# The up-projection of a conv-FFN by one level of Strassen's scheme, on an input that is normed first, with two tensors sent through DRAM

## Chip, cores and metric

One of the eight cores of a Trainium2 chip runs the whole program as one launch. The metric is the device time of one execution in microseconds, median of the runs; the profile is of one further execution. A core has TensorE (matmuls, PE below; its weight loads are listed apart as PEld), VectorE (DVE), ScalarE (ACT), GpSimd (POOL) and SyncE (SP), whose queue issues all of this kernel's DMAs. Each engine works through its own instruction list in order and waits on semaphores.

## The reference, cut to what matters

One decoder layer for 512 prompt tokens and 8 x 8 sample tokens that share all weights, 576 columns in all (`NT`). After four mixers, `w_out` and a cross-attention comes the FFN; this is the part that changes:

```python
def conv_ffn(xn, buf, w_up, conv_w, w_down):
    hup = xn @ w_up                                  # 2048 -> 11264 = 2 x 5632
    hc, new_buf = causal_dwconv(hup, buf, conv_w)    # width 3, along the tokens
    u, g = jnp.split(hc, 2, axis=-1)
    return (jax.nn.silu(g) * u) @ w_down, new_buf    # 5632 -> 2048

f, ffn_buf_new = conv_ffn(rmsnorm(x, lp['g_ffn']), ffn_buf, lp['w_up'], lp['ffn_conv_w'], lp['w_down'])
x = x + f
y = rmsnorm(x, g_final)
```

All inputs are fp32.

## The kernel before, in words

Activations lie transposed: 128 channels on the partitions, 576 tokens along the row. To keep fp32 accuracy in fp32r matmuls, each operand is split into a rounded half `hi` (ScalarE, L123) and a remainder `lo` (VectorE, L124, `lo = raw - hi`), and a product is three matmuls: hi by hi, hi by lo, lo by hi. A matmul has 128 x 128 weights and 288 moving columns, half of the tokens, so a 128 x 128 block of a weight array costs 6 matmuls (`linear`, L151). Weights come as tiles `raw` of 512 KB (512 rows by 256 columns, L119), in two buffers, and their halves in two buffers each.

The program is written once, and a scheduler orders each engine's instructions ahead of time by levels of priority (`at("evac")`, `at("weights")`, `at("drain")`, `at("mix")`, `at("fill")`, from high to low). What the chip runs is that fixed order.

The stages that matter here are these. `cross` ends with two halves of `w_mem_o`, whose sums are added to x in SBUF (`xT`, L303). In the second half `add_x("g_ffn")` also makes the FFN's input `xh`, `xl` (x times the gain; L305, L306) and sums the squares for the norm (ScalarE squares, GpSimd adds, L310). The factor 1/rms, `self.r`, is made by `row_rstd` (L323 to L329) and is applied later: `conv` multiplies each 128 x 576 result of `w_up` by it as it leaves PSUM (L507, L508). So the matmuls of `w_up` need not wait for the norm.

`ffn` goes over 11 blocks of 4 x 128 channels of u and of g. `up` makes 256 columns of u, then 256 of g; `conv` adds the state columns (GpSimd, L510), copies out the new state (GpSimd, L515, L516) and does the width-3 convolution (L521, L523); silu(g) u is split into the halves `mh`, `ml` (L332, L333), which stay in SBUF. `down(blk - 1)` is scheduled behind `up(blk)`: 16 column blocks x 4 x 6 matmuls, added to `xT` (L303). The last 4 channel blocks of `w_down` are done in `final` together with the last norm and the output (L602, L604).

PSUM has 8 banks: two accumulators `acc` of two banks each and four single banks.

Of the kernel before, what the change touches and what calls it, by code (L numbers as in the profile page):

```python
# [284 lines left out]
class Post(Net):  # L285
    def add_x(self, g=None, first=False):

        nc = self.nc
# [171 lines left out]
    def ffn(self):  # L460
        nc, tc, a, o = self.nc, self.tc, self.a, self.o
        NB = 4
        ah, al = {}, {}
# [2 lines left out]
        def down(blk):
            self.linear(ah.pop(blk), al.pop(blk), a["w_down"][0], 0, 2048, self.add_x(), k0=NB * blk, nk=NB)

        n = 44 // NB
        with ExitStack() as c:  # L470
            fp = c.enter_context(tc.tile_pool(name="fp", bufs=2, side="right"))
            f1 = c.enter_context(tc.tile_pool(name="f1", bufs=1, side="right"))
            st = f1.tile([128, 88, 16], F32, name="st")
            with self.at("mix"):

                raw = fp.tile([128, 1408], F32, name="sraw", bufs=1)
                nc.sync.dma_start(raw, bass.AP(tensor=a["state_ffn_conv"].tensor, offset=0, ap=[[1408, 8], [11264, 16], [1, 1408]]))
                s4 = st.rearrange("p (g j) r -> p g j r", g=8)
                for q in range(0, 11, 4):
                    m = min(4, 11 - q)  # L480
# [1 line left out]
                    for j in range(m):
                        nc.tensor.transpose(p[:, 128 * j:128 * j + 128], raw[:, 128 * (q + j):128 * (q + j) + 128], self.ident)
                    for j in range(m):
                        nc.vector.tensor_copy(s4[:, :, q + j], p[:, 128 * j:128 * j + 128].rearrange("p (g r) -> p g r", g=8))
            bufs = [f1.tile([128, 594], F32, name=f"ub{i}") for i in range(4)]
            for b in bufs:
                nc.gpsimd.memset(b, 0.0)
            outs, full = {}, []

            def states(ready):

                with self.at("fill"):
                    for g in ready:
                        p = self.pm()
                        nc.tensor.transpose(p[:72, :128], outs[g].rearrange("p r f -> p (r f)"), self.ident)
                        w = fp.tile([72, 128], F32, name="cw", bufs=2)
                        nc.scalar.copy(w, p[:72, :128])
                        for n, z in (("p_ffn_conv", w[:8]), ("s_ffn_conv", w[8:])):
                            nc.sync.dma_start(rows(n)[:, 512 * g:512 * g + 512].rearrange("r (f c) -> r f c", f=4), z)  # L500

            def conv(ft, ps, slot):

                u = bufs[slot]
                smp = u[:, 514:594].rearrange("p (b t) -> p b t", b=8)
                with self.at("evac"):
                    nc.vector.tensor_tensor(u[:, 2:514], ps[:, :512], self.r[:, :512], op=OP.mult)  # L507
                    nc.vector.tensor_tensor(smp[:, :, 2:10], ps[:, 512:].rearrange("p (b t) -> p b t", b=8),  # L508
                                            self.r[:, 512:].rearrange("p (b t) -> p b t", b=8), op=OP.mult)
                nc.gpsimd.tensor_copy(smp[:, :, 0:2], st[:, ft].rearrange("p (b t) -> p b t", b=8))  # L510
                g = ft // 4
                if ft % 4 == 0:
                    outs[g] = fp.tile([128, 18, 4], F32, name="co", tag=f"co{slot // 2}", bufs=2)
                co = outs[g]
                nc.gpsimd.tensor_copy(co[:, 0:2, ft % 4], u[:, 512:514])  # L515
                nc.gpsimd.tensor_copy(co[:, 2:18, ft % 4].rearrange("p (b t) -> p b t", b=8), smp[:, :, 8:10])  # L516
                if ft % 4 == 3:
                    full.append(g)
                y = fp.tile([128, 592], F32, name="y", tag=f"y{slot // 2}", bufs=2 - slot // 2)
                w = lambda k: self.v("ffn_conv_w", 88 * k + ft)  # L520
                nc.scalar.activation(y, u[:, :592], AF.Copy, scale=w(0))  # L521
                for k in (1, 2):
                    nc.vector.scalar_tensor_tensor(y, u[:, k:k + 592], w(k), y, op0=OP.mult, op1=OP.add)  # L523
                return y

            def up(blk):
                h, l = ah.setdefault(blk, {}), al.setdefault(blk, {})
                for pair in range(0, NB, 2):
                    ys = {}

                    def done_u(i, ps):
                        ys[i] = conv(NB * blk + pair + i, ps, i)

                    def done_g(i, ps):
                        j = NB * blk + pair + i
                        y = conv(44 + j, ps, 2 + i)
                        s = fp.tile([128, 592], F32, name="s", bufs=1)
                        nc.scalar.activation(s, y, AF.Silu)
                        t = fp.tile([128, NT], F32, name="t", bufs=1)
                        yu = ys[i]  # L540
                        nc.vector.tensor_tensor(t[:, :512], s[:, :512], yu[:, :512], op=OP.mult)
                        v = [z[:, 512:592].rearrange("p (b t) -> p b t", b=8)[:, :, 2:10] for z in (s, yu)]
                        nc.vector.tensor_tensor(t[:, 512:].rearrange("p (b t) -> p b t", b=8), v[0], v[1], op=OP.mult)
                        h[pair + i] = self.wo.tile([128, 604], F32R, name="mh", tag="mh", bufs=6)[:, :NT]
                        l[pair + i] = self.wo.tile([128, 604], F32R, name="ml", tag="ml", bufs=6)[:, :NT]
                        self.halves(h[pair + i], l[pair + i], t)
                    ready, full[:] = full[:], []
                    self.linear(self.xh, self.xl, a["w_up"][0], 128 * (NB * blk + pair), 256, done_u)
                    states(ready)
                    self.linear(self.xh, self.xl, a["w_up"][0], 5632 + 128 * (NB * blk + pair), 256, done_g)  # L550

            for blk in range(n):
                up(blk)
                if blk < n - 1 and blk:
                    down(blk - 1)
            down(n - 2)
            states(full)
        return ah.pop(n - 1), al.pop(n - 1)

    def final(self, fh, fl, fw, fo):  # L560

        nc, a, o = self.nc, self.a, self.o
# [5 lines left out]
        for c in range(0, 2048, 256):
            with self.at("weights"):
                raw = fw.tile([128, 4, 256], F32, name="raw", bufs=2)  # L570
                nc.sync.dma_start(raw, w[5120:, c:c + 256].rearrange("(k p) c -> p k c", p=128))
                nc.scalar.copy(wh[:, :, c:c + 256], raw)
# [1460 lines left out]
```

## Time and profile before

| | us |
|---|---|
| median of 3 runs (lowest, highest) | 3131.99 (3126.44, 3134.4) |
| the profiled execution's own time | 3129.54 |
| its span, from the first to the last instruction | 3127.7 |
| PE busy in the span | 3010.8 (96%) |
| DVE busy | 1715.1 (55%) |
| ACT busy | 962.6 (31%) |
| POOL busy | 437.0 (14%) |

A matmul is counted busy from its start to its modelled end, and matmuls overlap, so the rate of work is read from counts per stretch. The FFN runs from 1414 us (the first matmul of `w_up`) to 3055 us, `final` from there to the end. The granted TensorE clock is 0.988 of full speed over the span.

### The profile page before, as it was taken

To read this page: it belongs to the slowest core of one execution; us is meant where nothing else is said; L and a number is where in the kernel's file an instruction comes from. 1 tells how busy PE (TensorE), PEld (TensorE's weight loads), DVE (VectorE), ACT (ScalarE), POOL (GpSimd) and SP (SyncE) were. 2 spreads that over 40 slices of the span, in tenths; PEclk is the share of its full clock that TensorE was granted. 3 is DMA by queue.
4 is the path that set the end of the run, shared out by engine and by line. 5 is a ranking of instruction groups with operands and counts; after the bars stand their busy time and mean duration, and the time that the engine had idled before them with its cause. 6 is when DMAs were issued, how large, how long until landed. Compare 5 with 4: busy or idle time off the path is not lost.

```text
span 3127.7 us, 53649 instructions
## 1 busy us (share of the span) xinstructions
PE 3010.8 (96%) x22323; PEld 2867.6 (92%) x22323; DVE 1715.1 (55%) x2878; ACT 962.6 (31%) x1612; POOL 437.0 (14%) x563
## 2 busy tenths in 40 slices
PE   8998989999999999989999999999999999999998
PEld 8888977887888789879999999999999999999997
DVE  7857766778666666465443434444444444444454
ACT  4433322343332444233221222222222222222233
POOL 4111422313211003021110100000000000000000
PEclk9999999999999999999999999999999999999999
DMA  5455566545575553322222222222222222222232
GB/s 165 136 182 156 169 179 183 150 149 160 166 222 156 189 185 113 108 77 82 82 83 83 88 82 82 82 89 81 83 82 89 82 83 81 89 82 82 82 123 75
DMA packets 350587, 368.28 MB, mean 118 GB/s; under 512 B 35846, under 2 KB 298715, under 8 KB 349640
## 3 DMA queue, kind: packets, MB, share of 16 engines
q1 hardware_dynamic: 350344, 364.84, 37.3%
q8 instruction: 176, 2.88, 0.4%
q14 instruction: 67, 0.55, 0.1%
HBM read 320.44 MB, written 46.99 MB: 117 GB/s over the span
## 4 chain that ended last, share of the span: by engine, by line
PE 80%; DVE 8%; DMA 7%; issue 2%; ACT 1%; SPq 1%; POOL 1%; DVEq 0%; ACTq 0%; POOLq 0%
PE acc L151 68%; PE acc L602 2%; DVE lo L129 2%; DMA old<-in_cache_win_k 1%; PE acc L194 1%; PE pm L1395 1%; DMA od<-acc 1%; PE pm L926 1%; DMA kn<-in_cache_win_k 1%; DVE acc L877 1%; DMA raw<-in_w_down 1%; DMA old<-in_cache_win_v 1%; PE pm L805 1%; DMA dw<-dn 0%; DMA raw<-in_w_in 0%
## 5 line engine op out<-in xcount | busy, mean ns | idle before, releaser
L151 PE MATMUL acc<-xh,hi 128*128 128x288 f32 x4224 | 921.2, 299 | 20.3 <-DVE nt L1055 13.8
L151 PE MATMUL acc<-xl,hi 128*128 128x288 f32 x4224 | 923.3, 298 | 2.7 <-DVE xl L245 2.7
L151 PE MATMUL acc<-xh,lo 128*128 128x288 f32 x4224 | 914.9, 299 | 2.9 <-DVE lo L129 2.8
L124 DVE TENSOR_TENSOR lo<-raw,hi 128x1024 fp32r<-128x1024 f32 x322 | 397.2, 1233 | 594.6 <-ACT hi L123 588.1
L151 PEld LDWEIGHTS acc<-xh,hi 128*128 128x128 f32 x4224 | 686.0, 190 | 33.0 <-issue 25.1
L151 PEld LDWEIGHTS acc<-xl,hi 128*128 128x128 f32 x4224 | 687.6, 190 | 10.6 <-issue 6.8
L151 PEld LDWEIGHTS acc<-xh,lo 128*128 128x128 f32 x4224 | 684.0, 190 | 10.3 <-issue 4.9
L123 ACT CAST hi<-raw 128x1024 fp32r<-128x1024 f32 x322 | 337.9, 1049 | 1093.0 <-PE acc L151 1002.2
L151 PE MATMUL acc<-mh,hi 128*128 128x288 f32 x1920 | 421.7, 300 | 8.3 <-DVE xT L303 7.1
L151 PE MATMUL acc<-mh,lo 128*128 128x288 f32 x1920 | 416.9, 297 | 0.2 <-DVE lo L124 0.2
L151 PE MATMUL acc<-ml,hi 128*128 128x288 f32 x1920 | 416.0, 296 | 0.0
L303 DVE TENSOR_TENSOR xT<-acc,xT 128x576 f32<-128x576 f32 x240 | 181.2, 756 | 275.4 <-PE acc L151 274.8
L151 PEld LDWEIGHTS acc<-mh,hi 128*128 128x128 f32 x1920 | 308.3, 189 | 17.0 <-DVE xT L303 8.5
L151 PEld LDWEIGHTS acc<-ml,hi 128*128 128x128 f32 x1920 | 310.1, 189 | 3.9 <-issue 3.2
L151 PEld LDWEIGHTS acc<-mh,lo 128*128 128x128 f32 x1920 | 309.0, 189 | 3.5 <-issue 2.9
L515 POOL COPY co<-ub 128x2 f32<-128x2 f32 x88 | 61.0, 694 | 1291.3 <-DVE ub L507 1291.3
L128 ACT ACTIVATE hi<-raw,gmix 128x256 fp32r<-128x256 f32 x320 | 136.5, 498 | 212.2 <-PE acc L151 160.0
L129 DVE SCALAR_TENSOR_TENSOR lo<-raw,gmix,hi 128x256 fp32r<-128x256 f32 x320 | 171.9, 582 | 45.7 <-ACT hi L128 45.1
L523 DVE SCALAR_TENSOR_TENSOR y<-ub,vec,y 128x592 f32<-128x592 f32 x176 | 146.4, 832 | 42.6 <-ACT y L521 40.3
L521 ACT ACTIVATE y<-ub,vec 128x592 f32<-128x592 f32 x88 | 69.7, 792 | 157.9 <-DVE ub L508 156.0
L507 DVE TENSOR_TENSOR ub<-acc,sq 128x512 f32<-128x512 f32 x88 | 60.6, 688 | 53.9 <-PE acc L151 53.9
L1395 PE MATMUL pm<-dw 128*128 128x128 f32 (+1 forms) x456 | 61.8, 282 | 9.0 <-DVE dw L1409 5.3
(645 smaller groups left out, 2770.7 us busy)
## 6 DMA issues: line engine op xcount, KB each, us to landing
raw<-in_w_up SPq DMA_DIRECT2D x176, 512.0 KB
raw<-in_w_down SPq DMA_DIRECT2D x88, 512.0 KB
raw<-in_w_in SPq DMA_DIRECT2D x80, 512.0 KB
raw<-in_w_out SPq DMA_DIRECT2D x32, 512.0 KB
old<-in_cache_win_k SPq DMA_DIRECT2D x48, 256.0 KB
old<-in_cache_win_v SPq DMA_DIRECT2D x48, 256.0 KB
kn<-in_cache_win_k SPq DMA_DIRECT2D x32, 256.0 KB
v<-in_cache_win_v SPq DMA_DIRECT2D x32, 256.0 KB
```

Of the source, the lines that this page charges most:

```text
L123: nc.scalar.copy(hi, raw)
L124: nc.vector.tensor_tensor(lo, raw, hi, op=OP.subtract)
L128: nc.scalar.activation(hi[:, k], raw[:, k], AF.Copy, scale=g)
L129: nc.vector.scalar_tensor_tensor(lo[:, k], raw[:, k], g, hi[:, k], op0=OP.mult, op1=OP.subtract)
L151: nc.tensor.matmul(acc[m][:, 224 + 288 * j:512 + 288 * j], wt[:, k, 128 * m:128 * m + 128], at(x, kb + k)[:, 288 * j:288 * j + 288], start ...
L303: nc.vector.tensor_tensor(x, ps, old, op=OP.add)
L507: nc.vector.tensor_tensor(u[:, 2:514], ps[:, :512], self.r[:, :512], op=OP.mult)
L515: nc.gpsimd.tensor_copy(co[:, 0:2, ft % 4], u[:, 512:514])
L521: nc.scalar.activation(y, u[:, :592], AF.Copy, scale=w(0))
L523: nc.vector.scalar_tensor_tensor(y, u[:, k:k + 592], w(k), y, op0=OP.mult, op1=OP.add)
L602: nc.tensor.matmul(ps, x[k][:, tok], z[:, k, cs], start=k == 0 and i == 0, stop=k == 3 and i == 2)
L1395: nc.tensor.matmul(p[:n, n * h:n * h + n], lhs[:, h], rhs[:, h], start=True, stop=True)
```

## The change: what it does

`w_up` is multiplied by one level of Strassen's scheme (in the form with shared sums). A group is 2 row blocks x 2 column blocks of `w_up` (128 x 128 each) by 2 row blocks x 2 token halves of the input; 8 products of 128 x 128 x 288 become 7. The 7 products of each group accumulate in PSUM over the 8 groups of a 256-column pair, so the sums of products are done once a pair. One product is still three matmuls.

- `add_x(out=True)` no longer makes `xh`, `xl`; it writes each block of x to DRAM (`xd`) and sums the squares.
- `ffn_x` (new) starts when `self.r` is there: it reads x back (`z`), multiplies by gain and 1/rms, makes the four sums of the input blocks (three on GpSimd, one on VectorE) and splits all 7 operands, `Xh[q]`, `Xl[q]`, which stay in SBUF.
- `up_pair` (new) replaces `linear` for `w_up`: of each `raw` tile GpSimd makes the four sums `S` (4 instructions of 128 x 256); the halves are made in three pieces of 512, 256 and 1024 columns (`ah`/`al` from `raw`, `hi`/`lo` from `S`). The seven accumulators take seven banks: two `acc` and three of the four single banks; the fourth is left for the states. After the last of four chunks, ScalarE copies P1 (`t1`) and VectorE makes the four results (L538 to L544, and `sums`, L607 to L610), straight into the convolution's buffers `ub`, without the factor 1/rms.
- silu(g) u goes to DRAM (`hx`, one DMA of 288 KB per block), not into halves.
- `ffn_down` (new) runs after all of `w_up`: 5 blocks of 8 channel blocks, each read back (`ht`, three buffers) and split; before it x is read back into a new `xT`. The last 4 are split for `final`, whose weights are now made in `final_weights` at the end of `ffn_down`.

The diff, cut to its core:

```diff
-    def add_x(self, g=None, first=False):
+    def add_x(self, g=None, first=False, out=False):
...
-            if g:
+            if out:
+                nc.sync.dma_start(self.xd[m], x)
+            elif g:
                 nc.scalar.activation(self.xh[:, m], x, AF.Copy, scale=self.v(g, m))
...
+    def ffn_x(self, xc, zs):
...
+        for q in range(8):
+            with self.at("evac"):
+                z = zs.tile([128, 2, NT], F32, name="z", bufs=2)
+                nc.sync.dma_start(z, self.xd[2 * q:2 * q + 2].rearrange("k p t -> p k t"))
+                for k in range(2):
+                    nc.vector.scalar_tensor_tensor(z[:, k], z[:, k], self.v("g_ffn", 2 * q + k), self.r, op0=OP.mult, op1=OP.mult)
+                t = zs.tile([128, 4, 288], F32, name="t", bufs=2)
+                b11, b12, b21, b22 = (z[:, k, 288 * j:288 * j + 288] for k in range(2) for j in range(2))
+                sub(nc.gpsimd, t[:, 0], b12, b11)
+                sub(nc.gpsimd, t[:, 1], b22, t[:, 0])
+                sub(nc.vector, t[:, 2], b22, b12)
+                sub(nc.gpsimd, t[:, 3], t[:, 1], b21)
+                h, l = self.Xh[q], self.Xl[q]
+                self.halves(h[:, 0], l[:, 0], b11)
+                self.halves(h[:, 1:3].rearrange("p a b -> p (a b)"), l[:, 1:3].rearrange("p a b -> p (a b)"), z[:, 1])
+                self.halves(h[:, 3:], l[:, 3:], t)
+    def up_pair(self, sp, w, c0, done):
+        prods = {"P1": (("a", 0), 0), "P2": (("a", 1), 1), "P4": (("a", 2), 6), "P5": (("s", 0), 3), "P6": (("s", 1), 4), "P7": (("s", 2), 5), "P3": (("s", 3), 2)}
+        for ch in range(4):
+            with self.at("weights"):
+                raw = self.wp.tile([128, 4, 256], F32, tag="raw", name="raw", bufs=2)
...
+                g = nc.gpsimd.tensor_tensor
+                g(S[:, 0], A(2, 1), A(2, 2), op=OP.add)
+                g(S[:, 1], S[:, 0], A(1, 1), op=OP.subtract)
+                g(S[:, 2], A(1, 1), A(2, 1), op=OP.subtract)
+                g(S[:, 3], A(1, 2), S[:, 1], op=OP.subtract)
...
+                self.halves(ah[:, :2], al[:, :2], both)
+                self.halves(ah[:, 2], al[:, 2], A(2, 2))
+                self.halves(sh, sl, S)
...
+                        for j, (wt, xx) in enumerate(((hi, xh), (hi, xl), (lo, xh))):
+                            nc.tensor.matmul(P[name], wt[:, i, q], xx, start=ch == 0 and q == 0 and j == 0, stop=ch == 3 and q == 1 and j == 2)
+                if ch == 3:
+                    with self.at("evac"):
...
+                            nc.vector.tensor_tensor(u2, t1, P["P6"], op=OP.add)
...
+                            nc.vector.tensor_tensor(t1, u2, P["P7"], op=OP.add)
+                            done(0, 1, OP.subtract, t1, P["P4"])
+                            done(1, 1, OP.add, t1, P["P5"])
+                            nc.vector.tensor_tensor(u2, u2, P["P5"], op=OP.add)
...
+                nc.sync.dma_start(self.hx[j + n], t)
...
+        for blk in range(5):
+            ps = [parts(NB * blk + k, hp, 11) for k in range(NB)]
+            self.linear({k: p[0] for k, p in enumerate(ps)}, {k: p[1] for k, p in enumerate(ps)}, a["w_down"][0], 0, 2048, self.add_x(), k0=NB * blk, nk=NB)
```

How the instructions stand. First VectorE's list in the middle of the FFN. Before, one 256-column half of u (`ub` is the convolution's buffer, `lo` the weights' remainder, line numbers those of the kernel before):

```order
L507 TENSOR_TENSOR ub_15175<-acc,sq 128x512
L508 TENSOR_TENSOR ub_15175<-acc,sq 128x8x8
L523 SCALAR_TENSOR_TENSOR y<-ub_15175,vec,y 128x592 x2
L507 TENSOR_TENSOR ub_15176<-acc,sq 128x512
L508 TENSOR_TENSOR ub_15176<-acc,sq 128x8x8
L124 TENSOR_TENSOR lo<-raw,hi 128x1024
L523 SCALAR_TENSOR_TENSOR y<-ub_15176,vec,y 128x592 x2
L124 TENSOR_TENSOR lo<-raw,hi 128x1024 x3
```

After the change, the end of one pair and the start of the next (line numbers of the changed kernel; L337 is `halves`, `pp` and `acc` are the products in PSUM):

```order
L538 TENSOR_TENSOR u_21630<-t_21603,pp 128x288
L607 TENSOR_TENSOR ub_15312<-t_21603,acc 128x288
L541 TENSOR_TENSOR t_21603<-u_21630,pp 128x288
L337 TENSOR_TENSOR al<-raw,ah 128x512
L337 TENSOR_TENSOR al<-raw,ah 128x256
L607 TENSOR_TENSOR ub_15313<-t_21603,acc 128x288
L609 TENSOR_TENSOR ub_15313<-t_21603,acc 128x224
L610 TENSOR_TENSOR ub_15313<-t_21603,acc 128x8x8
L544 TENSOR_TENSOR u_21630<-u_21630,acc 128x288
L337 TENSOR_TENSOR lo<-S,hi 128x1024
L609 TENSOR_TENSOR ub_15312<-u_21630,pp 128x224
L610 TENSOR_TENSOR ub_15312<-u_21630,pp 128x8x8
```

The weights' remainder is in three pieces per chunk, and instructions on sums in PSUM stand between the pieces of the next pair's second chunk.

Second, VectorE at the start of the FFN. Before, the last evacuations of `w_mem_o` and the norm stand among the FFN's first weights:

```order
L303 TENSOR_TENSOR xT<-acc,xT 128x576
L306 SCALAR_TENSOR_TENSOR xl<-xT,vec,xh 128x576
L124 TENSOR_TENSOR lo<-raw,hi 128x1024
L306 SCALAR_TENSOR_TENSOR xl<-xT,vec,xh 128x576
L124 TENSOR_TENSOR lo<-raw,hi 128x1024
L324 TENSOR_SCALAR nt<-pm 128x288 x2
L326 RECIPROCAL sq<-nt 128x288 x2
```

After the change, the norm (L328 to L333, which are L324 to L329 before), and then the input's operands (`z`, `t`, `Xl`) among the first weights (`al`, `lo`):

```order
L333 SCALAR_TENSOR_TENSOR sq<-nt,sq 128x288 x2
L337 TENSOR_TENSOR al<-raw,ah 128x512
L337 TENSOR_TENSOR al<-raw,ah 128x256
L337 TENSOR_TENSOR al<-raw,ah 128x512
L337 TENSOR_TENSOR al<-raw,ah 128x256
L478 SCALAR_TENSOR_TENSOR z<-z,vec,sq 128x576 x2
L337 TENSOR_TENSOR Xl_15151<-z,Xh_15150 128x288
L472 TENSOR_TENSOR t<-z 128x288
L478 SCALAR_TENSOR_TENSOR z<-z,vec,sq 128x576 x2
L337 TENSOR_TENSOR Xl_15151<-z,Xh_15150 128x576
L337 TENSOR_TENSOR lo<-S,hi 128x1024
```

The DMA of the first `z` waits for the last instruction of the norm, since its buffer takes the place of the norm's own buffers.

Third, the SP queue where `w_up` ends and `w_down` begins. Before, the two kinds of weights alternate:

```order
L119 DMA raw<-in_w_up 128x4x256 x9
L119 DMA raw<-in_w_down 128x4x256 x3
L500 DMA out_p_ffn_conv<-cw 2x4x128
L500 DMA out_s_ffn_conv<-cw 16x4x128
L119 DMA raw<-in_w_down 128x4x256
```

After the change, the last two blocks of silu(g) u, the four parts of x, and the blocks that are read back:

```order
L627 DMA hx<-t 128x576
L2098 DMA xT<-xd 128x4x576 x4
L627 DMA hx<-t 128x576
L638 DMA ht<-hx 128x576 x12
L119 DMA raw<-in_w_down 128x4x256
```

The read-back of x stands ahead of the last write of `hx` and of every read of `ht`. Its first DMA waits for the last instruction that reads the last `ub` (L600), and the first `ht` waits until the last write of `hx` has landed and the last silu is done, by the places of the buffers in SBUF.

## Rows read from the trace of the kernel before

**Rows 1.** Page: span, and the busy time of each engine.

```profile
span 3127.7 us, 53649 instructions
PE 3010.8 (96%) x22323; PEld 2867.6 (92%) x22323; DVE 1715.1 (55%) x2878; ACT 962.6 (31%) x1612; POOL 437.0 (14%) x563
```

**Rows 2.** Windows: length, busy us (count) of PE, PEld, DVE, ACT, POOL; clock, DMA, GB/s.

```profile
1430.00:3000.00 1570.00, 1570.00 (x11819) 1569.67 (x11818) 676.44 (x867) 384.05 (x437) 114.54 (x258) 1.00 0.26 84
```

**Rows 3.** Chain that ended last, 1774 to 1928 us: start, us, link.

```profile
1780.72 146.68 PE acc L151 x1104
```

**Rows 4.** Groups by shape, 1430 to 3000 us: count, busy, mean ns, idle before.

```profile
L151 PEld LDWEIGHTS acc<-xh,hi 128*128 128x128 f32 x2780 | 447.8, 189 | 0.0
...
L124 DVE TENSOR_TENSOR lo<-raw,hi 128x1024 fp32r<-128x1024 f32 x246 | 301.3, 1225 | 565.6 <-ACT hi L123 561.1
L523 DVE SCALAR_TENSOR_TENSOR y<-ub,vec,y 128x592 f32<-128x592 f32 x174 | 144.7, 832 | 42.6 <-ACT y L521 40.3
L333 DVE TENSOR_TENSOR ml<-t,mh 128x576 fp32r<-128x576 f32 x42 | 31.7, 755 | 6.6 <-ACT mh L332 6.6
L541 DVE TENSOR_TENSOR t<-s,y 128x512 f32<-128x512 f32 x42 | 28.9, 689 | 10.3 <-ACT s L538 10.0
L508 DVE TENSOR_TENSOR ub<-acc,sq 128x64 f32<-128x64 f32 x87 | 18.7, 215 | 0.0
L328 DVE TENSOR_TENSOR nt<-nt 128x288 f32<-128x288 f32 x1 | 0.5, 451 | 0.0
L510 POOL COPY ub<-st 128x16 f32<-128x16 f32 x84 | 16.9, 201 | 176.3 <-DVE y L523 176.3
```

**Rows 5.** Timeline of VectorE, 3009 to 3012 us: start, us, instruction.

```profile
3010.05 1.22 DVE L124 TENSOR_TENSOR lo<-raw,hi 128x1024 fp32r<-128x1024 f32 x1
3011.18 0.75 DVE L303 TENSOR_TENSOR xT<-acc,xT 128x576 f32<-128x576 f32 x1
```

**Rows 6.** Groups of GpSimd by shape, 60 to 95 us.

```profile
L1535 POOL TENSOR_TENSOR cm<-W 128x256 f32<-128x256 f32 x1 | 1.1, 1084 | 0.0
L1534 POOL TENSOR_TENSOR cm<-W,W 128x256 f32<-128x256 f32 x1 | 0.7, 658 | 0.1
```

**Rows 7.** Timelines of VectorE and GpSimd, 349 to 364 us, both without a pause.

```profile
351.30 5.20 DVE L129 SCALAR_TENSOR_TENSOR lo<-raw,gmix,hi 128x256 fp32r<-128x256 f32 x4
363.71 0.49 DVE L129 SCALAR_TENSOR_TENSOR lo<-raw,gmix,hi 128x256 fp32r<-128x256 f32 x1 [0.33 <-ACT hi L128]
...
350.08 6.13 POOL L1897 TENSOR_TENSOR nt<-xh,xl 128x576 f32<-128x576 f32 x4 [1.50 <-DMA xd<-nt]
```

**Rows 8.** Windows: second half of `w_mem_o`, and a piece of it behind a wait.

```profile
1373.70:1414.40 40.70, 31.03 (x189) 29.22 (x190) 35.19 (x41) 22.55 (x34) 23.69 (x21) 0.88 0.20 58
1383.30:1386.90 3.60, 3.60 (x17) 3.60 (x16) 2.93 (x8) 0.58 (x1) 1.90 (x5) 0.50 0.01 2
```

**Rows 9.** Timelines from 1386 to 1433 us, GpSimd, PE and VectorE: squares, then the norm.

```profile
1390.84 1.43 POOL L310 TENSOR_TENSOR sq<-sq,nt 128x576 f32<-128x576 f32 x1 [0.64 <-ACT nt L308]
...
1422.24 1.13 PE L323 MATMUL pm<-sq,mean 128*128 128x288 f32 x4
...
1428.13 0.67 DVE L485 COPY st<-pm 128x128 f32<-128x128 f32 x3
...
1429.65 1.22 DVE L124 TENSOR_TENSOR lo<-raw,hi 128x1024 fp32r<-128x1024 f32 x1
...
1431.16 0.82 DVE L329 SCALAR_TENSOR_TENSOR sq<-nt,sq 128x288 f32<-128x288 f32 x2
```

**Rows 10.** Timelines of SP's queue and ScalarE, 3001 to 3007 us: a weight load and its reader.

```profile
3002.06 1.94 SPq L571 DMA_DIRECT2D raw<-in_w_down  x2
...
3005.74 1.05 ACT L572 CAST wh<-raw 128x1024 fp32r<-128x1024 f32 x1 [2.98 <-DMA raw<-in_w_down]
```

**Rows 11.** Windows of the first loads; the last number is GB/s.

```profile
3.00:5.00 2.00, 0.18 (x1) 0.08 (x1) 0.00 (x0) 0.17 (x1) 0.00 (x0) 1.00 0.87 328
11.00:13.00 2.00, 2.00 (x17) 2.00 (x15) 1.71 (x3) 1.60 (x4) 1.92 (x2) 1.00 1.04 434
```

More of the change, by code (lines that the diff above doesn't have):

```diff
@@ L456, in cross @@
             z = lambda y: {k: y[2 * pair + k] for k in range(2)}
-            self.linear(z(oh), z(ol), a["w_mem_o"][0], 0, 2048, self.add_x("g_ffn" if pair else None), k0=2 * pair, nk=2)
+            self.linear(z(oh), z(ol), a["w_mem_o"][0], 0, 2048, self.add_x(out=pair > 0), k0=2 * pair, nk=2)
         self.banks = (0, 1, 2, 3)
[L460 to L463, printed above, removed]
-        rows = lambda n: o[n].rearrange("a b k c -> (a b k) c")
[L466 to L480, printed above, removed]
-                    p = self.pm()
[L482 to L558, printed above, removed]
@@ L560, in final @@
-    def final(self, fh, fl, fw, fo):
+    def ffn_x(self, xc, zs):
+        nc = self.nc
+        B11, B21, B22, T1, T2, T3, T4 = range(7)
+        self.Xh, self.Xl = {}, {}
+        for q in range(7, -1, -1):
+            self.Xh[q] = xc.tile([128, 7, 288], F32R, name=f"Xh{q}")
+            self.Xl[q] = xc.tile([128, 7, 288], F32R, name=f"Xl{q}")
+        sub = lambda e, o, x, y: e.tensor_tensor(o, x, y, op=OP.subtract)
+        for q in range(8):
[14 more added lines that the diff above has]
+                self.halves(h[:, 3:], l[:, 3:], t)
@@ new lines, in ffn_down, with parts @@
+    def ffn_down(self, hp, hs, last):
+        nc, a = self.nc, self.a
+        NB = 8
+        def parts(j, pool, bufs):
+            with self.at("drain"):
+                t = hs.tile([128, NT], F32, name="ht", bufs=3)
+                nc.sync.dma_start(t, self.hx[j])
+                h, l = (pool.tile([128, NT], F32R, name=f"h{z}", bufs=bufs) for z in "hl")
+                self.halves(h, l, t)
+                return h, l
+        for blk in range(5):
+            ps = [parts(NB * blk + k, hp, 11) for k in range(NB)]
+            self.linear({k: p[0] for k, p in enumerate(ps)}, {k: p[1] for k, p in enumerate(ps)}, a["w_down"][0], 0, 2048, self.add_x(), k0=NB * blk, nk=NB)
+        ps = [parts(40 + k, last, 4) for k in range(4)]
+        return [p[0] for p in ps], [p[1] for p in ps]
@@ new lines, in final_weights @@
+    def final_weights(self, fw):
+        nc = self.nc
+        w = self.a["w_down"][0]
+        self.wh = fw.tile([128, 4, 2048], F32R, name="wh")
+        self.wl = fw.tile([128, 4, 2048], F32R, name="wl")
+        for c in range(0, 2048, 256):
+            with self.at("weights"):
+                raw = self.wp.tile([128, 4, 256], F32, tag="raw", name="raw", bufs=2)
+                nc.sync.dma_start(raw, w[5120:, c:c + 256].rearrange("(k p) c -> p k c", p=128))
+                nc.scalar.copy(self.wh[:, :, c:c + 256], raw)
+                nc.vector.tensor_tensor(self.wl[:, :, c:c + 256], raw, self.wh[:, :, c:c + 256], op=OP.subtract)
@@ L562, in final @@
+    def final(self, fh, fl, fo):
         nc, a, o = self.nc, self.a, self.o
-        w = a["w_down"][0]
-        wh = fw.tile([128, 4, 2048], F32R, name="wh")
-        wl = fw.tile([128, 4, 2048], F32R, name="wl")
+        wh, wl = self.wh, self.wl
         g = fo.tile([128, 2048], F32, name="gB")
         nc.sync.dma_start(g, bass.AP(tensor=a["g_final"].tensor, offset=0, ap=[[0, 128], [1, 2048]]))
[L568 to L572, printed above, removed]
-                nc.vector.tensor_tensor(wl[:, :, c:c + 256], raw, wh[:, :, c:c + 256], op=OP.subtract)
@@ L1991, in run @@
                     self.row_rstd()
-                fh, fl = self.ffn()
-            with pool("fw") as fw, pool("fo", **R) as fo:
-                self.banks = (0, 1, 2, 3)
-                self.final(fh, fl, fw, fo)
+            late.close()
+            self.banks = (3,)
+            with pool("xc", **R) as xc, pool("sp") as sp:
+                with pool("zs") as zs:
+                    self.ffn_x(xc, zs)
+                with pool("f1") as f1, pool("fp") as fp:
+                    self.ffn_up(sp, fp, f1)
+            self.banks = (0, 1, 2, 3)
+            fw = post.enter_context(pool("fw", **R))
+            self.xT = post.enter_context(pool("xq")).tile([128, 16, NT], F32, name="xT")
+            with self.at("mix"):
+                for k in range(0, 16, 4):
+                    nc.sync.dma_start(self.xT[:, k:k + 4], self.xd[k:k + 4].rearrange("k p t -> p k t"))
+            with pool("hs") as hs, pool("hp", **R) as hp:
+                fh, fl = self.ffn_down(hp, hs, fw)
+                self.final_weights(fw)
+            self.final(fh, fl, post.enter_context(pool("fo")))
 _OUTS = [
```

109 lines of the change are left out of this document (107 added, 2 removed).

## The prediction

> **What bounds the kernel now.** I read the page first: PE is busy in 96% of the span, no other engine in more than 55% [rows 1]. Busy time of overlapping matmuls is not work, so next the windows. From 1430 to 3000 us PE ends 11,819 matmuls in 1570.0 us, 132.8 ns each, without a gap, while DVE is busy 43% of the time and POOL 7% [rows 2]. The chain of waits says the same: a link of 1104 matmuls in 146.68 us, 132.9 ns each, and nine such follow each other, with short pieces of 48 matmuls between them [rows 3]. So the FFN before is PE work end to end; a matmul that goes there gives back 0.133 us as long as nothing else becomes later than PE. The change therefore is two questions: how many matmuls go, and what waits it opens.
>
> **1. Matmuls: -140.3 us.** `w_up` has 16 x 88 blocks at 6 matmuls, 8448. With 7 products of 8 there are 7392, and 1056 x 0.1328 us = 140.3 us. Per 256-column pair PE needs 168 x 0.1328 = 22.3 us instead of 25.5. `w_down` keeps its matmuls. Weight loads cost nothing extra: there is a load for each matmul already (11,818 for 11,819) and it is hidden [rows 2].
>
> **2. The 44 pairs: does anything need more than 22.3 us? +13 us.** VectorE does per pair 4 chunks of 1024, 512 and 256 columns. 1.225 and 0.689 us are rows [rows 4]; the 256 follow from their slope (1.05 ns a column), 0.42; together 4 x 2.33 = 9.3 us. The convolution is 4 x 0.832 = 3.3. The sums from PSUM are 5 of 288 columns at 0.45 and two pairs of 224 and 64 (0.38 by the slope, and 0.215), 3.4 us. silu(g) u is 0.9 on average. Sum 17.0 us in 27 instructions; since the next one starts 0.09 us before the profile's end of the last (1.13 after a 1.22 [rows 5]), about 14.6 us of VectorE's time. ScalarE does the first half of each split, as VectorE the second, and less besides, so it comes behind VectorE. GpSimd, nearly free before, gets 16 sums of 128x256, 0.66 us each when hardly disturbed, up to 1.08 [rows 6], and 6 copies of about 0.20 [rows 4]: 11.8 us.
>
> The last two engines get in each other's way. Where GpSimd adds two SBUF tensors back to back, each VectorE instruction of 0.49 us with two SBUF inputs takes 1.30, and a GpSimd add, 1.43 by itself [rows 9], comes every 1.53 [rows 7]. So they take turns, but not with their whole length: 1.43 + (0.49 - 0.09) would be 1.83, the turn is 1.53, so 0.30 overlaps. A GpSimd sum then holds VectorE up for at most 0.66 - 0.30 = 0.36 us. Sixteen of them: 5.8 us, VectorE 20.4 us. That is under 22.3, with 1.9 to spare for its waits on ScalarE's first convolution step and on the last products. Where the pair ends, the order gives slack: the sums are followed by P3 and by the next pair's P6, P1 and P2 on PE before the accumulator of P4 and P5 is written again, some 40 matmuls or 5 us, and VectorE frees it about 3 us after the pair's end. I take 0.3 us per pair, 13 us. Bounds: 0, and 44 us, 1 us a pair, if hand-overs and waits in VectorE's order come to 2.9 us a pair instead of less than 1.9.
>
> The Trainium skill, "SBUF — State Buffer", section "SBUF: two separate sides", says of this pair of engines that whoever starts first holds the shared ports for its whole instruction and the other is blocked. The trace agrees with the blocking, not with the whole length: of 1.83 us, 1.53 are left [rows 7].
>
> **3. Before the first pair: +34 us.** Now `w_mem_o`'s second half takes 40.7 us for 192 matmuls [rows 8], since a state load, a clock at 0.50 behind that wait, and two VectorE instructions per block hold it up. After the change VectorE has one of 0.75 per 1.6 us of matmuls and the state load stands later, so 192 x 0.1328 = 25.5 us, a gain of 15.2. Then PE must wait, which it does not now. From its last matmul: evacuation 0.75 [rows 5], square (taken like VectorE's instruction on as many columns, 0.75), GpSimd's add 1.43, three hand-overs of 0.2: 3.5 us. From the mean's matmul to the finished norm 1431.98 - 1422.24 = 9.7, of which 1.9 are foreign [rows 9]: 7.8. The first `z` is issued only then; a 512 KB load takes 3.7 us to its reader [rows 10]. So VectorE starts on the operands 15.0 us after PE's last matmul.
>
> Per q it has 2 x 0.83, 2 x 0.45, 0.755 and 1.36 (1152 columns by the slope): 4.7 us, 8 times 37.4; the first weights among them 9.5; less 59 x 0.09: 41.6 us. GpSimd has 24 sums of 288 and about 16 of 256 columns there; each holds VectorE up by 0.36 to 0.4. All of VectorE's instructions there read two SBUF tensors, so I take 10 of the possible 16 us: 52 us. About 4 us of matmuls follow the last operand. PE thus ends the first pair 15 + 52 + 4 = 71 us after `w_mem_o`, where 22.3 us are its work: 49 idle, less the 15.2 gained, +34. Bounds: no collision +24, all +40. (At half clock, as in the 17 matmuls of 3.6 us [rows 8], the pair's 168 matmuls need 36 us and still hide in this.)
>
> **4. Between `w_up` and `w_down`: +28 us.** Before, nothing: blocks of both alternate. Now, after the last product, VectorE does two sums from PSUM, a weight piece, the convolution and silu product of two blocks, with ScalarE's steps between: by the same rows about 9.3 us until the last `ub` is read. Only then are the four loads of x issued, 4.72 MB; bulk loads move 328 to 434 GB/s [rows 11], 12.5 us and 2 to land: 23.8. The last `hx` block (VectorE ready at 11) is queued behind them, lands at about 25, and the first `ht` another 2.2 later, 27.2; ScalarE's and VectorE's halves at 0.755 each [rows 4] with hand-overs: 28.9. Three buffers at 4 us a round (load 2.2, two steps, hand-overs) bring the eighth block at 37.7. PE, which works on each as it comes, ends the first 96 matmuls (12.8 us of work) at some 41. Loss 28 us; 19 if `hx` and `ht` do not queue behind x, 33 if the 2.2 are the 3.7 of [rows 10]. Behind that `w_down` runs at PE's rate as before, with half as many evacuations. `final` has the same matmuls; I put it at 0.
>
> **Sum.** -140.3 + 13 + 34 + 28 = -65 us. The profiled execution took 3129.5, so 3064.5 for its like; the median of the runs is 2.5 higher: **3067 us**, 2.1% faster.
>
> **Rivals.** A: VectorE and GpSimd become the bound. If their turns do not overlap (16 x 0.66 + 1.2 on top of VectorE's 14.6) a pair takes 26.4; if half of that hides behind the sums from PSUM, 25. The change loses once a pair takes more than 22.3 + (140.3 - 62) / 44 = 24.1 us; at 25 it is 3132 - 140 + 62 + 119 = 3173, at 26.4 3234. For it: the 1.30 us of [rows 7], and sums up to 1.08 [rows 6]. Against: the 0.30 of overlap, and VectorE's instructions on PSUM. I give it 12 in 100. (The section of the Trainium skill named above, taken at its word, is this case.)
>
> B: the two gaps are smaller: the first operands come without collisions and the loads of x overlap the rest, no stall in the pairs: -140 + 24 + 19 = -97, 3035. For it: bulk loads at 434 GB/s. Against: a fixed order with each wait written in it. 18 in 100.
>
> C: the gaps are dearer and pairs stall by 1 us: -140 + 44 + 40 + 33 = -23, 3109. 15 in 100.
>
> D: the matmuls don't go at 0.133 us. Each block of weights now serves one run of 288 columns instead of two; if a load of 0.189 us [rows 4] set the rate, 7392 x (0.189 - 0.133) would add 414 us. Against it: as many loads as matmuls already, all hidden [rows 2]. 3 in 100.
>
> **How the numbers follow.** The forecast, 3045 to 3100, has 52 in 100. Range 3030 to 3120: it takes in B and C, and leaves out A and D and a rest. 0.3% of 3132 is 9.4 us, about what a measurement of this kernel tells from no change: faster means under 3122.6, slower over 3141.4. Faster: forecast 0.52, B 0.18, C 0.11, 0.81; same: C 0.04, A 0.02, 0.06; slower: A 0.10, D 0.03, 0.13.
>
> **What the profile after would show.** Step 1: 17,472 matmuls of 288 columns instead of 18,528, and 0.133 us each in stretches without waits. Step 2: a pair every 22.3 to 23 us, PE's idle time in the FFN's middle under 2%; if PE waits there on `al`, `lo` or `acc` for more than 1.8 us a pair, A is true. VectorE's pieces of weights would show means above 1.23, 0.69 and 0.42, by up to 0.36. Step 3: some 49 us of PE idle before and in the first pair, ended by `Xh`, `Xl`. Step 4: some 28 us idle before `w_down`, ended by `hh`, `hl` and, behind them, by the DMAs of x. The prediction is wrong if the pairs take over 24 us, or if either gap is twice what I say.

## The result, and the profile after

The changed kernel takes 3095.64 us (median of 4 runs, 3093.48 to 3103.04); the kernel before, run beside it, takes 3129.76. The ratio is 0.9894, with a 95% interval of 0.9871 to 0.9917. The change makes the kernel 34 us faster, 1.1%, where I had forecast 65.

The page of the profiled execution (3093.82 us), to be read beside [rows 1]: the span, and each engine's busy time, share and count.

```profile
span 3092.0 us, 53960 instructions
PE 2904.6 (94%) x21267; PEld 2744.4 (89%) x21267; DVE 2084.5 (67%) x3402; ACT 1127.7 (36%) x2016; POOL 1194.4 (39%) x1290
```

PE has 1056 matmuls less, as worked out. GpSimd has gone from 437 to 1194 us, and that is more than its new instructions should take.

The windows, one for each stage (columns as in [rows 2]): second half of `w_mem_o`; from there to the end of the first pair; pairs 2 to 44; from the last product of `w_up` until the 97th matmul of `w_down` starts; the rest of `w_down`; `final`.

```profile
1373.70:1399.10 25.40, 24.45 (x178) 23.58 (x176) 14.71 (x18) 11.76 (x17) 20.17 (x13) 1.00 0.58 205
1399.10:1484.40 85.30, 45.45 (x174) 36.70 (x172) 77.40 (x76) 31.56 (x48) 66.71 (x58) 0.60 0.30 97
1484.40:2473.90 989.50, 973.20 (x7256) 963.76 (x7256) 834.14 (x1170) 432.07 (x704) 814.95 (x939) 1.00 0.33 106
2473.90:2517.40 43.50, 15.49 (x100) 14.83 (x98) 18.25 (x30) 13.59 (x20) 0.68 (x4) 0.69 0.65 226
2517.40:3018.20 500.80, 500.80 (x3760) 500.80 (x3760) 181.95 (x192) 104.81 (x113) 0.00 (x0) 1.00 0.32 104
3018.20:3092.00 73.80, 62.73 (x307) 49.07 (x305) 36.25 (x70) 29.79 (x70) 0.00 (x0) 0.96 0.28 101
```

Against the steps of the prediction:

| stage | forecast, us | measured, us | difference |
|---|---|---|---|
| second half of `w_mem_o` | 25.5 | 25.4 | 0 |
| its last matmul to the first pair's end | 71 | 85.3 | +14 |
| pairs 2 to 44, each | 22.6 | 23.01 | +18 in 43 pairs |
| last product to the 97th matmul of `w_down` (forecast: 96 through) | 41 | 43.5 | +2.5 |
| `final` (72.5 before) | as before | 73.8 | +1.3 |

These come to 36 us too much. Some 4 us of them are transposes of the states among the pairs' matmuls: the window has 7256 matmuls, and 43 pairs are 7224 products. The forecast of 22.3 us left them out, but the kernel before has them too, so step 1 is no worse for them. The pitch of a matmul is as before, 0.1328 us (963.80 us for 7257 in e1's window below). The missing 30 us are thus in two places, the first pair and the 43 others, about half in each.

What PE waits for in pairs 2 to 44, from the waits view (total, times, longest), first at the matmuls, then at the weight loads ahead of them:

```profile
PE acc L528 <- ACT t L533: 13.0, 13, 1.5
PE pp L528 <- DVE u L538: 3.0, 8, 0.8
```

```profile
PEld acc L528 <- ACT t L533: 17.0, 17, 1.7
PEld pp L528 <- DVE u L538: 8.1, 19, 1.1
```

At the matmuls a wait counts only from the modelled end of the matmul before. The waits at the weight loads, 25.8 us with one of 0.7, are the whole excess of the pairs, 43 times 0.6. The largest part is not `al` or `lo`, which I had named, but the copy of P1 on ScalarE (L533), which lets the next pair's first products into the accumulator. One such wait, from timelines of PE, ScalarE, GpSimd and VectorE between 1658 and 1668 us:

```profile
1667.61 0.40 PE L528 MATMUL acc<-Xh,ah 128*128 128x288 f32 x1 [1.51 <-ACT t L533]
...
1666.21 1.04 ACT L336 CAST hi<-S 128x1024 fp32r<-128x1024 f32 x1 [4.10 <-POOL S L507]
1667.16 0.39 ACT L533 COPY t<-acc 128x288 f32<-128x288 f32 x1
...
1660.42 3.54 POOL L504 TENSOR_TENSOR S<-raw 128x256 f32<-128x256 f32 x1 [4.11 <-DMA raw<-in_w_up]
1663.93 0.73 POOL L506 TENSOR_TENSOR S<-raw 128x256 f32<-128x256 f32 x1
1664.62 0.73 POOL L505 TENSOR_TENSOR S<-S,raw 128x256 f32<-128x256 f32 x1
...
1665.45 0.73 POOL L507 TENSOR_TENSOR S<-raw,S 128x256 f32<-128x256 f32 x1
...
1659.73 0.82 DVE L600 SCALAR_TENSOR_TENSOR y<-ub,vec,y 128x592 f32<-128x592 f32 x1
1660.48 1.22 DVE L337 TENSOR_TENSOR lo<-S,hi 128x1024 fp32r<-128x1024 f32 x1
1661.62 0.68 DVE L624 TENSOR_TENSOR t<-s,y 128x512 f32<-128x512 f32 x1
1662.22 0.21 DVE L626 TENSOR_TENSOR t<-s,y 128x64 f32<-128x64 f32 x1
1662.35 1.02 DVE L337 TENSOR_TENSOR al<-raw,ah 128x512 fp32r<-128x512 f32 x2
```

Read it upwards. VectorE runs without a pause until 1663.37; the first sum of GpSimd, 0.73 us when nothing is in its way, starts at 1660.42 and ends 0.6 us after that run, 3.54 us long. The other sums follow, the last is ready at 1666.18, ScalarE's cast of S starts then, and the copy of P1, long ready to go, stands behind the cast. PE goes on at 1667.61. In pairs 2 to 44 seven of the first sums take 3.4 to 3.7 us, and each is followed 7 us later by one of the seven longest waits of PE (some 11 of the 25.8 us). The other waits for the copy, 5.9 us, also stand behind a cast that waits for GpSimd's last sum. Of the 19 waits for L538 ten of 0.3 us follow on such a cast; the other nine, 5.2 us, end a run of 17 VectorE instructions without a pause, with pieces of 1.24 and 1.75 us for 0.69 and 1.22. There VectorE itself, held up, is late.

The groups of GpSimd and of VectorE's weight pieces by shape (pairs 2 to 44, then 1500 to 2460 us) show both sides of the hold-up:

```profile
L505 POOL TENSOR_TENSOR S<-S,raw 128x256 f32<-128x256 f32 x169 | 200.4, 1186 | 0.0
L506 POOL TENSOR_TENSOR S<-raw 128x256 f32<-128x256 f32 x169 | 177.0, 1047 | 0.0
L504 POOL TENSOR_TENSOR S<-raw 128x256 f32<-128x256 f32 x169 | 173.0, 1024 | 140.0 <-DMA raw<-in_w_up 110.1 <-DVE al L337 12.5 <-DVE y L600 8.1
L507 POOL TENSOR_TENSOR S<-raw,S 128x256 f32<-128x256 f32 x169 | 161.1, 953 | 10.7
...
L337 DVE TENSOR_TENSOR lo<-S,hi 128x1024 fp32r<-128x1024 f32 x167 | 230.4, 1380 | 100.1 <-ACT hi L336 100.1
L337 DVE TENSOR_TENSOR al<-raw,ah 128x512 fp32r<-128x512 f32 x167 | 157.0, 940 | 3.9 <-ACT ah L336 3.6
L337 DVE TENSOR_TENSOR al<-raw,ah 128x256 fp32r<-128x256 f32 x166 | 127.7, 770 | 0.0
```

VectorE's pieces are 0.16, 0.25 and 0.35 us longer than 1.23, 0.69 and 0.42, as forecast. But a sum of GpSimd takes 1.05 us in the mean instead of 0.66, so GpSimd is busy not 11.8 but 19.0 us of 23.

In the first pair VectorE is busy from 1411.13 to 1480.56 without a pause. Some of its instructions there, first held up, then alike ones in a short time in which GpSimd has nothing to do:

```profile
1431.01 2.48 DVE L478 SCALAR_TENSOR_TENSOR z<-z,vec,sq 128x576 f32<-128x576 f32 x2
1433.41 1.88 DVE L337 TENSOR_TENSOR Xl<-t,Xh 128x1152 fp32r<-128x1152 f32 x1
1435.21 0.98 DVE L337 TENSOR_TENSOR Xl<-z,Xh 128x288 fp32r<-128x288 f32 x1
...
1439.58 1.34 DVE L337 TENSOR_TENSOR Xl<-z,Xh 128x576 fp32r<-128x576 f32 x1
...
1443.95 0.45 DVE L472 TENSOR_TENSOR t<-z 128x288 f32<-128x288 f32 x1
...
1445.45 0.75 DVE L337 TENSOR_TENSOR Xl<-z,Xh 128x576 fp32r<-128x576 f32 x1
1446.12 1.35 DVE L337 TENSOR_TENSOR Xl<-t,Xh 128x1152 fp32r<-128x1152 f32 x1
1447.39 0.81 DVE L478 SCALAR_TENSOR_TENSOR z<-z,vec,sq 128x576 f32<-128x576 f32 x1
```

Each shape is 0.4 to 0.6 us longer when held up. At the undisturbed lengths, less 0.09 us for each start before the end of the last, the 63 instructions are about 43 us of work; they took 69.4. Behind that VectorE's first sum of products (L607) stands 3.4 us for GpSimd's memset of `ub` (L568), which comes after the late sums, and PE 0.5 us for that.

### The profile page after: what moved, and what is told of

Read it like the earlier page. It is cut to its first block, busy times and chain, and to the rows that moved or that the text cites. A ratio compares the mean times of both kernels' runs of the same rounds, so it can differ in the third digit from the quotient of the medians.

```text
span 3092.0 us, 53960 instructions
## 1 busy us (share of the span) xinstructions
PE 2904.6 (94%) x21267; PEld 2744.4 (89%) x21267; DVE 2084.5 (67%) x3402; ACT 1127.7 (36%) x2016; POOL 1194.4 (39%) x1290
## 5 line engine op out<-in xcount | busy, mean ns | idle before, releaser
L528 PE MATMUL acc<-Xh,ah 128*128 128x288 f32 x1056 | 317.1, 301 | 28.5 <-ACT Xh L336 14.9
L151 PE MATMUL acc<-xh,hi 128*128 128x288 f32 x1408 | 320.0, 307 | 20.0 <-DVE nt L1148 13.8
L528 PE MATMUL acc<-Xl,ah 128*128 128x288 f32 x1056 | 315.8, 299 | 9.6 <-DVE Xl L337 9.4
L151 PE MATMUL acc<-xl,hi 128*128 128x288 f32 x1408 | 321.2, 306 | 2.5 <-DVE xl L245 2.5
L151 PE MATMUL acc<-xh,lo 128*128 128x288 f32 x1408 | 319.6, 306 | 3.7 <-DVE lo L129 3.7
L528 PE MATMUL pp<-Xh,hi 128*128 128x288 f32 x1056 | 314.4, 300 | 3.5 <-DVE u L538 3.0
L528 PE MATMUL acc<-Xh,al 128*128 128x288 f32 x1056 | 315.6, 299 | 0.0
L337 DVE TENSOR_TENSOR lo<-S,hi 128x1024 fp32r<-128x1024 f32 x176 | 243.1, 1381 | 100.9 <-ACT hi L336 100.9
L337 DVE TENSOR_TENSOR al<-raw,ah 128x512 fp32r<-128x512 f32 x352 | 288.4, 856 | 4.7 <-ACT ah L336 4.5
L151 PEld LDWEIGHTS acc<-xh,hi 128*128 128x128 f32 x1408 | 233.4, 194 | 32.8 <-issue 24.7
L151 PEld LDWEIGHTS acc<-xl,hi 128*128 128x128 f32 x1408 | 235.2, 194 | 10.4 <-issue 6.8
L151 PEld LDWEIGHTS acc<-xh,lo 128*128 128x128 f32 x1408 | 234.4, 194 | 10.6 <-issue 4.9
```

The lines of the kernel that those rows point to most:

```text
L151: nc.tensor.matmul(acc[m][:, 224 + 288 * j:512 + 288 * j], wt[:, k, 128 * m:128 * m + 128], at(x, kb + k)[:, 288 * j:288 * j + 288], start ...
L337: self.nc.vector.tensor_tensor(lo, src, hi, op=OP.subtract)
L528: nc.tensor.matmul(P[name], wt[:, i, q], xx, start=ch == 0 and q == 0 and j == 0, stop=ch == 3 and q == 1 and j == 2)
```

## The experiments

Theory A: GpSimd's sums and VectorE's instructions hold each other up, which stretches VectorE in the first pair and makes the sums late in the others. Its rivals are named with each run. Until the last matmul of `w_mem_o` the work is the same in all kernels, yet in these single runs that matmul ends between 1398 and 1411 us; so stages are read from there, and whole times of single runs are good to some 6 us.

**e1: no sums.** The four sums of the weights are left out; the raw tile is split in their place.

```diff
-                g(S[:, 0], A(2, 1), A(2, 2), op=OP.add)
...
-                self.halves(sh, sl, S)
+                self.halves(sh, sl, raw...)
```

> This kernel leaves out the four sums S of each weight tile on GpSimd: ScalarE and VectorE split the raw tile itself in their place, so P3, P5, P6 and P7 multiply the wrong blocks; all other instructions stay. Theory A (GpSimd and VectorE hold each other up): in the first pair each GpSimd instruction costs VectorE about 0.55 us (69.4 us measured for 43.0 us of undisturbed work, 48 instructions), so 24 fewer give VectorE's stretch 13 us back, 69 to 56; in pairs 2 to 44 no cast of S is late any more, TensorE's waits of 19 us and the half clock behind them go, 23.0 us a pair become 22.5; whole time near 3060. Rival B2 (the weight tile itself comes late, two raw buffers): the cast then waits for the load instead, pairs stay at 22.9 to 23.0, time near 3082.

Measured: 3061.52 us, pairs 22.41 us, first pair's end 74.1 us after `w_mem_o`. Windows of VectorE's stretch before the first pair's end and of pairs 2 to 44:

```profile
1415.40:1473.40 58.00, 34.88 (x151) 29.27 (x152) 53.38 (x61) 24.27 (x38) 26.57 (x24) 0.68 0.40 127
1475.80:2439.60 963.80, 963.28 (x7257) 962.56 (x7256) 663.61 (x1170) 437.66 (x704) 95.17 (x260) 1.00 0.35 109
```

PE's waits in the pairs are gone with the same two raw buffers and the same loads, so the weight tile's load by itself is not what was late. VectorE needs 15.4 us a pair, where it needed 19.4. (The half clock that this expectation names in the pairs is none: the granted clock there is 1.00 in both kernels; single starts behind a wait are 0.1 us slower.)

**e2: the sums on VectorE.**

```diff
-                g = nc.gpsimd.tensor_tensor
+                g = nc.vector.tensor_tensor
```

> The four sums S of each weight tile are made on VectorE instead of GpSimd. Theory A: VectorE takes 16 x 0.33 = 5.3 us more per pair by its rows and loses the 4.3 us by which its instructions are stretched now, so it needs about 20 of 22.4 us; no cast of S waits for GpSimd; pairs 22.5 to 22.6 instead of 23.0, first pair 24 x (0.55 - 0.33) = 5 us shorter; time near 3070. Rival C (VectorE's own load is what delays TensorE): pairs of 23.2 us or more, time 3095 or more.

Measured: 3077.97 us; pairs 22.45 us, first pair's end after 80.4 instead of 85.3 us. Pairs 2 to 44:

```profile
1491.80:2457.00 965.20, 964.79 (x7258) 963.69 (x7256) 884.28 (x1846) 438.93 (x705) 187.56 (x260) 1.00 0.35 109
```

VectorE is busier than in the changed kernel, 20.6 us a pair against 19.4, and PE waits less: 0.3 us in all. Rival C falls: VectorE's load was not it. The whole time is 8 us above the expectation, because `w_mem_o` ended 12 us later in this run.

**e3: the input's subtractions on VectorE,** the weights' sums left on GpSimd.

```diff
-                sub(nc.gpsimd, t[:, 0], b12, b11)
+                sub(nc.vector, t[:, 0], b12, b11)
```

> Only the three subtractions per q that make the input's operands move from GpSimd to VectorE (24 in all, before and in the first pair). Theory A: VectorE gains 24 x 0.36 = 8.6 us of its own work and loses 24 x 0.55 = 13.2 us of hold-ups: its stretch falls from 69.4 to about 65, pairs 2 to 44 stay at 23.0, time near 3089. Rival (the first pair is long because VectorE's own work was underestimated, not because of hold-ups): the stretch grows to 78, time near 3102.

Measured: 3101.82 us, which alone would speak for the rival; but `w_mem_o` ended 7 us later. VectorE's stretch is 66.0 us, not 78, the first pair ends after 81.8 us, the pairs stay at 23.05:

```profile
1418.30:1484.30 66.00, 39.66 (x156) 32.09 (x156) 62.33 (x87) 26.17 (x39) 38.52 (x25) 0.68 0.35 112
```

**e4: the copy of P1 on VectorE.**

```diff
-                            nc.scalar.copy(t1, P["P1"])
+                            nc.vector.tensor_copy(t1, P["P1"])
```

> Only the copy of P1 out of PSUM moves from ScalarE to VectorE, ahead of VectorE's last split of S in its order; on ScalarE it stands behind a cast that waits for GpSimd's last sum. Theory B (the order on ScalarE makes the late sum into a wait of TensorE): pairs 2 to 44 fall from 23.0 to 22.5 or 22.6, time near 3075. Theory A alone (GpSimd is late whatever stands behind it): the wait moves on to the next reader of a late S, pairs 22.8 to 23.0, time 3085 to 3094.

Measured: 3099.41 us, pairs 23.01; `w_mem_o` ended 3 us later. The waits moved on to the next instruction that stands behind a late cast:

```profile
PE pp L528 <- DVE u L538: 13.7, 17, 1.4
PE acc L528 <- DVE t L533: 2.8, 7, 0.6
```

So the order on ScalarE only decides who passes the delay on; with e1 and e2, where the waits go, the late sum is its source.

**e5: half of the sums on VectorE.**

```diff
-                g(S[:, 0], A(2, 1), A(2, 2), op=OP.add)
+                nc.vector.tensor_tensor(S[:, 0], A(2, 1), A(2, 2), op=OP.add)
...
-                g(S[:, 2], A(1, 1), A(2, 1), op=OP.subtract)
+                nc.vector.tensor_tensor(S[:, 2], A(1, 1), A(2, 1), op=OP.subtract)
```

> Of the four sums S of a weight tile the two that read only the raw tile (S0, S2) move to VectorE, the other two stay on GpSimd; the copy of P1 keeps its place on ScalarE behind a cast that waits for GpSimd. Theory A in the form that GpSimd's load makes it late (19.2 us busy of 23.0 a pair now): GpSimd falls to about 11 us, VectorE to 15.4 + 8 x 0.33 + 8 x 0.26 = 20.1, no cast is late, pairs 22.4 to 22.5. Rival: any one sum behind a run of VectorE instructions is stretched to 3 us and late, however little GpSimd has to do: TensorE's waits on the copy of P1 stay in part, pairs 22.7 to 22.9.

Measured: 3107.97 us, pairs 23.35 us: worse than either whole, and neither theory's number. GpSimd is down to 10.1 us a pair, and the waits for the copy of P1 are gone, as theory A says. But VectorE is at 20.5, as in e2, and PE now waits for VectorE's first sum of products; VectorE waits for the raw tiles:

```profile
PE pp L528 <- DVE u L538: 27.3, 28, 2.1
...
DVE S L504 <- DMA raw<-in_w_up: 109.2, 116, 2.2
```

In this kernel's order the S0 and S2 of a tile whose load is still awaited stand right ahead of L538 on VectorE in 42 of the 44 pairs, and in e2 behind it; in e2 VectorE waits 22.0 us for raw tiles, here 109.2. With the same busy time I take the order for the cause, but no run tested it alone: how much of the 0.9 us a pair is the order and how much the hand-overs between the two engines was not separated.

**e6: both kinds on VectorE** (the edits of e2 and e3).

> The weight sums S and the input's subtractions are all made on VectorE; GpSimd has no work with two SBUF inputs left in this stage. Theory A: VectorE's stretch before the first pair's end is its own work without hold-ups, 43.0 + 24 x 0.36 + 24 x 0.33 = 59.6 us instead of 69.4, the first pair ends 75 to 76 us after the last matmul of w_mem_o instead of 85.3, pairs 22.45. Rival (VectorE's work is what counts, hold-ups were mostly hidden): the stretch stays at 66 to 70 us. From the last matmul of w_mem_o to the end 1659 us instead of 1693; whole time 3060 to 3070, since that matmul came between 1399 and 1411 us in the runs so far.

Measured: 3063.35 us; pairs 22.46, first pair's end after 78.4 us, some 3 more than forecast: 28 sums of weights fall into VectorE's stretch, not 24, and it waits 1.3 us. VectorE's stretch:

```profile
1409.80:1473.10 63.30, 36.88 (x153) 31.10 (x154) 62.00 (x115) 26.44 (x40) 0.00 (x0) 0.66 0.37 117
```

The stretches of five kernels together, each one's own work taken at the undisturbed lengths (good to about 1 us):

| kernel | sums of GpSimd there | VectorE busy | own work | held up | per sum |
|---|---|---|---|---|---|
| changed | 48 | 69.4 | 42.7 | 26.7 | 0.56 |
| e1 | 24 | 53.4 | 40.4 | 13.0 | 0.54 |
| e2 | 24 | 65.7 | about 50 | 15 to 16 | 0.6 |
| e3 | 24 | 62.3 | 50.6 | 11.7 | 0.49 |
| e6 | 0 | 62.0 | 60.4 | 1.6 | |

The hold-up goes with the number of GpSimd's sums, 0.5 to 0.6 us each, whichever sums they are.

**e7: x at need.** The four loads of x go; the evacuations of `w_down`'s first block add x from small loads, as the first block of `w_out` does.

```diff
-                for k in range(0, 16, 4):
-                    nc.sync.dma_start(self.xT[:, k:k + 4], ...)
...
-                    old = self.nt()
+                    old = pool.tile([128, NT], F32, name="xo", bufs=2) if pool else self.nt()
```

> The read-back of x in four loads of 1.15 MB ahead of the last write of silu(g) u is taken out; the first block's evacuations add x from 16 loads of 288 KB each, two at a time, as they need it. The prediction's bound for the gap without x ahead in the queue was 9 us less: TensorE is through 96 matmuls 34 to 35 us after the last product of w_up instead of 43.5; whole time near 3085. Rival (the round of the three buffers, not the queue, sets when the eighth block is there): under 4 us less, 40 us or more.

Measured: 3089.36 us; the 97th matmul of `w_down` starts 34.8 us after the last product instead of 43.5. SP's queue in the changed kernel and, in the second fence, here:

```profile
2481.27 0.34 SPq L627 DMA_DIRECT2D hx<-t  x1
2483.03 2.13 SPq L2098 DMA_DIRECT2D xT<-xd  x4
2485.25 2.90 SPq L627 DMA_DIRECT2D hx<-t  x1
2497.76 1.28 SPq L638 DMA_DIRECT2D ht<-hx  x3
```

```profile
2484.16 3.64 SPq L627 DMA_DIRECT2D hx<-t  x2
2489.66 0.80 SPq L303 DMA_DIRECT2D xo<-xd  x2
2490.49 16.91 SPq L638 DMA_DIRECT2D ht<-hx  x12
```

From the last product (2473.9 and 2476.8) to the first read-back it was 23.9 us and is 13.7. The rival falls.

**e8: e6 and e7 together.**

> All sums and subtractions on VectorE, and x loaded at need. If the two places are independent, the gains add: 10 us before the first pair's end, 24 us in the pairs, 9 us between w_up and w_down, some 43 us less than the changed kernel: near 3052 us, 0.975 of the kernel before. Rival: 3066 or more, if VectorE, then busy over 20 of 22.4 us a pair, has its waits where another run had not.

Measured: 3057.12 us (3055.56 to 3061.75), 0.9765 of the kernel before (0.9751 to 0.9778): faster than the kernel before and than the changed kernel. The gains add: 8.4 us up to the first pair's end, 25.3 in the pairs and 9.9 behind them, 43.6 in all where 43 were expected. The whole time is 38.5 us shorter; in the profiled execution `w_mem_o` ended 5 us later than in that of the changed kernel. The pairs, and the stretch up to the 97th matmul of `w_down`:

```profile
1481.40:2445.60 964.20, 964.20 (x7257) 963.56 (x7255) 883.11 (x1845) 439.69 (x705) 189.10 (x260) 1.00 0.35 109
2445.60:2479.20 33.60, 14.91 (x100) 14.36 (x98) 17.85 (x29) 13.36 (x19) 0.69 (x4) 0.75 0.54 169
```

## Why the prediction was right, and where it was off

**Sign and range: right.** The forecast said faster by 65 us with a range that ends at 3120; the kernel is 34 us faster. That lies at the upper end of the likeliest case (3045 to 3100), on the side of rival C: a dearer gap and slower pairs. The size was off by nearly half: two terms, the pairs and the first pair, cost some 30 us more than put.

**Step 1, the matmuls: right.** 7392 instead of 8448, and pairs of 22.41 us where nothing is late (e1), so rival D is out: a change of weights for every run of 288 columns costs nothing.

**Step 2, the pairs: the term was mis-sized, and by the other engine of the pair.** "I take 0.3 us per pair" measured 0.60 (23.01 less the 22.41 of e1), 26 us instead of 13. The step asked whether VectorE fits into the pair. In the mean it does: I had put it at 20.4 us at most, it needs 19.4, and its pieces grew by what was forecast. Only 5.2 of the 26 us stand behind runs of VectorE that are late by themselves. I had left GpSimd at the 11.8 us of undisturbed sums; but a hold-up has two sides. GpSimd takes 19.0 us a pair, its sums come late, and the delay runs through ScalarE's cast, and from there mostly through the copy of P1, into PE. The slack "where the pair ends", worked out on VectorE, is then lost on ScalarE. Shown by e1 and e2 (no sums on GpSimd, no wait) and e4 (another place for the copy, same loss). Rival A, with VectorE and GpSimd as the bound at 24.1 us or more, did not come.

**Step 3, the first pair: right in mechanism, one term mis-sized.** The norm is there 11.2 us after the last matmul (11.3 forecast), and the operands start after 15.6 us (15.0). VectorE's own work in the 65.9 us from there is about 41 us (41.6), so the term "I take 10 of the possible 16 us" for collisions measured 25. GpSimd starts 44 sums there, not 40, each costs 0.5 to 0.6 us, not 0.36 to 0.4, and the discount from 16 to 10 is given no reason: all of VectorE's instructions there read two SBUF tensors, as the step itself says. The price rested on a misreading of [rows 7]. The four VectorE instructions in 5.20 us are one of 0.49, not held up, and three of 1.64 or 1.65, not four of 1.30. Two of the three, from the kernel before:

```profile
351.71 1.65 DVE L129 SCALAR_TENSOR_TENSOR lo<-raw,gmix,hi 128x256 fp32r<-128x256 f32 x1
353.28 1.64 DVE L129 SCALAR_TENSOR_TENSOR lo<-raw,gmix,hi 128x256 fp32r<-128x256 f32 x1
```

The turn is thus 1.57 us, and a GpSimd add of 1.43 costs VectorE 1.57 less 0.40 (0.49 less 0.09), 1.17 us: 0.26 overlaps, not 0.30. A sum of 128x256 takes 0.73 us by itself in the changed kernel, not 0.66. Less 0.26 that is 0.47 a sum, not far from what was measured. The Trainium skill, "SBUF — State Buffer", section "SBUF: two separate sides", says that the engine that starts first keeps the shared ports for its whole instruction. The trace lies between that and my price, 0.55 of 0.73 us. The clock of 0.60 in this stretch hides behind VectorE, as put.

**Step 4, between `w_up` and `w_down`: right, in part by luck.** The last `ub` was read at 9.0 us (9.3 forecast), PE's first matmul came at 27.6 (the first `h` at 28.9), and 96 were through at 42.6 (41); the 97th started at 43.5, 0.9 us of it a wait for a cast of weights. No row shows the 2 us that x takes to land or the 2.2 us of a load of 288 KB. The first read-back was issued at 23.9 us, not at about 25, and its reader on ScalarE started 3.1 us behind (2500.82), not 2.2: two misses that nearly cancel. Without x in the queue the loss falls by 8.7 us, where 28 less 19 had been put as the bound (e7).

**What was left at nothing:** the rest of `w_down` takes 500.8 us for 3760 matmuls, 0.1332 us each where the kernel before has 0.1328, and `final` is 1.3 us longer than before; why is not known.

## What to carry to other kernels

When work goes to an engine that holds up a busy one, as GpSimd does with VectorE here, add the hold-up to both lists, and ask of the less busy engine too what comes late and who stands behind it in order. A third engine that only passes a late result on (here a copy behind a cast) looks like the cause in the waits view; follow the rows back to the instruction that is longer than its like. Two inputs of one queue that the next stage needs in turn, here x and the read-back, are worth a look at which is needed first.
